# Merged products of the gate and up projections, and tiles moved to multiples of 512 bytes, in a two-layer hybrid decoder trunk

## The chip, the cores and the metric

The kernel runs on one core of one Trainium2 chip. The metric is device time in microseconds, as the median of several runs. The kernel before was measured three times. All matrix work runs on TensorE, called PE in the profile, whose weight loads are listed apart as PEld. VectorE is DVE, ScalarE is ACT, GpSimd is POOL, and SP issues the transfers of the weights.

## What is computed

The reference is a trunk of two layers over 256 tokens of width 1024, in float32. Each layer is a half-weighted SwiGLU, a mixer and another half-weighted SwiGLU, each behind an RMS norm. The four feed-forward parts, each with a hidden width of 2816, are where the change works:

```
def swiglu(h, w_gate, w_up, w_down):
    return (jax.nn.silu(h @ w_gate) * (h @ w_up)) @ w_down

for layer in range(DEPTH):
    x = x + FFN_RES * swiglu(rms_norm(x, pre_norm[layer]), pre_w_gate[layer], ...)
    h = rms_norm(x, mix_norm[layer])
    x = x + (ssd_mla_mixer(h, ...) if layer % 2 == 0 else swa_gla_mixer(h, ...))
    x = x + FFN_RES * swiglu(rms_norm(x, post_norm[layer]), post_w_gate[layer], ...)
```

Mixer 0 joins a state-space scan with latent attention, mixer 1 a sliding-window attention with gated linear attention.

## The kernel before

**Two parts for every operand.** A float32 value is held as two float32r parts, hi (the value rounded by a cast on ACT) and lo (the rest, a subtraction on DVE). A product of an activation h and a weight w is the sum of three matmuls: h-hi by w-hi, h-lo by w-hi and h-hi by w-lo. Each matmul has a weight load of its own on TensorE (the stationary operand, 128 by 128) and then a moving operand whose columns stream through.

**The weights** come in the order of their use through `Stream.load` (line 68). Each slot is a tile of 128 partitions by up to 1024 columns, 512 KB: SP starts its transfer into one of 4 raw buffers, ACT casts it into one of 8 hi buffers (line 78), and DVE subtracts into one of 8 lo buffers (line 80). POOL takes a third of the subtractions where a share is given (line 82), which the loop over column tiles and the down projection of the feed-forward part don't do.

**A feed-forward part** is `ffn` (line 340). The first 512 columns of gate and up are made by tokens (`in_tok`, lines 274 to 276): the stationary operand is a 128-token block of the activations and the moving operand 512 columns of the weight. The other 18 column tiles of 128 columns each go through `in_ch` (lines 284 to 293): the stationary operand is a 128 by 128 block of the weight, the moving operand all 256 tokens. For each of the 8 k tiles, `in_ch` issues hi by xh, hi by xl and lo by xh, into one half of a PSUM bank; gate has one half and up the other, so a column tile fills one of the 4 banks that products with weights take in turn. Then ACT takes the silu of the gate half (line 364), DVE multiplies by the up half (line 365), and `split` makes the two parts of the result on ACT (line 229) and DVE (line 230). The down projection is `proj` (line 295): for each of the 22 k tiles the stationary operand is a block of activations and the moving one 512 columns of the weight, three matmuls (lines 308 to 310) for each of two token tiles and two halves. After the first token tile ends, its norm runs under the second one's products (`norm`, line 243); `split` there works on four k tiles at once, 512 elements to a partition. The turned result is hT, two tiles of hi (four k tiles each) and two of lo.

**Order.** The engines' queues are in order. A scheduler sets the order from the program and a timing model, so a piece that waits holds what stands behind it on its engine.

**Place of the tiles in SBUF.** A pool lays its tiles one after another. Before, the pool "sb" holds everything but the weights, large and small tiles mixed, and the pool of the weights follows it. In the built program every large tile of group "b" (hT, gains, x, half of the lo parts of the hidden activations) and every raw, hi and lo weight buffer begins 128 bytes past a multiple of 512. The large tiles of group "a" (the hi parts of the hidden activations and the others of the lo parts, the outputs of the attention, the turned outputs of the scan) begin 192 bytes past one. A 128 by 128 float32r block is 512 bytes to a partition, and blocks lie at steps of 512 bytes within these tiles, so a stationary block has the start of its tile: 128 past for the weights' blocks and for hT, 192 past for the hidden activations.

Of the kernel before, what the change touches and what calls it, by code (L numbers as in the profile page):

```python
# [6 lines left out]
dt = mybir.dt  # L7
# [21 lines left out]
# log1p(e) / e on [0, 1], least maximum relative error 5e-9  # L29
# [4 lines left out]
# columns of the row of small vectors that is broadcast to all partitions  # L34
# [7 lines left out]
# columns of the square constants  # L42
# [3 lines left out]
def two_pi_parts():  # L46
    """2 pi as 12-bit pieces and the rest"""
    parts, rest = [], TWO_PI
    for _ in range(3):
        m, e = np.frexp(rest)  # L50
        p = float(np.ldexp(np.floor(m * 4096), e - 12))
        parts.append(p)
        rest -= p
    return parts + [rest]


class Stream:
    """The weights in the order of their use. Each slot is [128, w]; a load
    brings one or two slots in one transfer, and each is split exactly into
    two float32r parts."""  # L60
# [7 lines left out]
    def load(self, widths, share=0.0):  # L68
        """share: of the subtractions, the part that Pool takes over from DVE"""
# [18 lines left out]
class Net:  # L88
    def __init__(self, tc, sb, wp, ps, args):
        self.tc, self.nc = tc, tc.nc  # L90
        self.sb, self.ps, self.args = sb, ps, args
        self.st = Stream(self.nc, wp, args["w"], 4, 8)
        self.k = 0

# [5 lines left out]
    def blk(self, shape, name, dtype=F32, grp="b"):  # L100
        """a tile from the common pools; those of a group are given out in the order of the program,
        so that work that may run ahead of other work has a group of its own"""
        size = int(np.prod(shape[1:])) * 4
        tag, bufs = next((t, n) for t, m, n in self.POOLS[grp] if size <= m)
        return self.sb.tile(shape, dtype, tag=tag, name=f"{name}_{self.uid()}", bufs=bufs)
# [4 lines left out]
    def bank(self, shape, name):  # L110
        """for the products with weights"""
# [11 lines left out]
    def order(self, later, earlier):  # L123
        """both on one engine: `later` is issued after `earlier`"""
# [15 lines left out]
    def constants_more(self):  # L140
# [13 lines left out]
        # the silu of the convolution is taken as (tanh(v / 2) + 1) * (v / 2): halves, exactly  # L154
        nc.vector.tensor_scalar(out=self.conv, in0=self.conv, scalar1=0.5, scalar2=None, op0=ALU.mult)
        # gains of the no-position part of q and k, on k alone
# [3 lines left out]
        # masks added to scores in PSUM  # L160
        self.identb = self.small([P, P], "identb", BF16)
# [8 lines left out]
        # distances of the window's positions, with a large number outside of it  # L170
# [61 lines left out]
    def power(self, out, in_):  # L232
        """in_ ** -0.5"""
        self.pow = self.nc.gpsimd.tensor_tensor(out=out, in0=in_, in1=self.mhalf[:, :in_.shape[1]], op=ALU.pow)

    def new_hT(self):
        return [[self.blk([P, 4, S], f"hT{s}{j}", F32R) for j in range(2)] for s in "hl"]

    @staticmethod
    def hk(hT, k):  # L240
        return hT[0][k // 4][:, k % 4, :], hT[1][k // 4][:, k % 4, :]

    def norm(self, x, t, g, hT):
        """token tile t of the RMS norm of x, turned: columns of t in hT"""
# [10 lines left out]
        for h in range(2):  # L255
# [5 lines left out]
            c = (slice(None), slice(None), slice(t * P, (t + 1) * P))  # L261
            self.split(hT[0][h][c], hT[1][h][c], tp)
# [3 lines left out]
    def mm_tok(self, out, at, ks, t, w, first, last):  # L266
        """out[tokens of t, cols] += a^T w over the k tiles ks, w their (hi, lo)"""
# [10 lines left out]
    def in_tok(self, out, hT, t, w, n, per):  # L278
        """out = h w for token tile t; w: slots of `per` k tiles, n columns each"""
# [4 lines left out]
    def in_ch(self, out, hT, w):  # L284
        """out [128 columns of the weight, 256 tokens]"""
# [8 lines left out]

    def proj(self, nk, at, x, scale, after, turn=TURN, lag=LAG, share=0.0):
        """x[t] += scale * (a w), a = at(k, t) (hi, lo) [128, 128]. The first token tile ends `lag`
        k tiles before the second, so that after(t, half) runs under the second's products; what
        TensorE has to do in it is put between these from their half `turn` on."""
# [33 lines left out]
        # at the end of all the second tile ends by halves  # L332
# [7 lines left out]
    def ffn(self, hT, x, after):  # L340
# [17 lines left out]
        for f in range(G0, NF):  # L358
            w = st.load([D, D])
            b = self.bank([P, 2, S], "gu")  # L360
            for j in range(2):
                self.in_ch(b[:, j, :], hT, w[j])
            sg = self.blk([P, n0], "sg")[:, :S]
            nc.scalar.activation(out=sg, in_=b[:, 0, :], func=AF.Silu)
            nc.vector.tensor_tensor(out=sg, in0=sg, in1=b[:, 1, :], op=ALU.mult)  # L365
# [8 lines left out]
    def log1p_exp(self, v, e, name):  # L374
        """e = log1p(exp(-|v|)); returns the tile that holds it"""
# [10 lines left out]
    def attend(self, t, pt, v, den, out):  # L386
        """out: (hi, lo) [128, 4, 128] of the turned outputs of 8 heads;
        pt(block, h) [128 k, 128 q], v(block, h) [128 k, 64]"""
# [14 lines left out]
    def turn_probs(self, p, n, name):  # L403
        """p(h) [128 q, 128 k] for 8 heads -> [128 k, 8, 128 q]"""
# [13 lines left out]
    def conv_silu(self, c, b, out):  # L418
        """causal convolution and silu of channel tile c, b [128, 256] in PSUM"""
# [11 lines left out]
    def apply_rope(self, out, x, t, which, nh):  # L431
        """out, x [128, nh, 2, 16] (out may not be x)"""
# [9 lines left out]
    def mixer0(self, hT, x, after):  # L442
# [3 lines left out]
        # --- dt, q_a, kv_c, k_pe, by tokens  # L446
# [33 lines left out]
        # --- B and C of the state space, [state, token]  # L480
# [9 lines left out]
        # --- q and k of the latent attention  # L490
# [5 lines left out]
        for t in range(2):  # L496
# [15 lines left out]
            # 96^-1/2 / rms = (sum of squares + 96 eps)^-1/2  # L512
# [40 lines left out]
        # --- dt = softplus, a = -dt exp(a_log), its running sum by chunk  # L553
        e = self.small([P, 2, 16], "dte")
        l1 = self.log1p_exp(dtv, e, "dtl")
        dts = self.small([P, 2, 16], "dts")
# [10 lines left out]
        # the same by rows, to come back on all partitions  # L567
# [12 lines left out]
        # --- scores and softmax  # L580
# [33 lines left out]
        # --- decays of a chunk, masked products C B  # L614
        dec = self.small([P, 16], "dec")

        def decays(t):
# [10 lines left out]
            for g in range(4):  # L628
# [3 lines left out]
                if t == g == 0:  # the rows arrive while DVE still has a convolution to do  # L632
# [10 lines left out]
        # --- x of the state space: by tokens, times dt and times D  # L643
# [21 lines left out]
        # --- outputs of the scan onto x D  # L665
# [10 lines left out]
        # --- gate, by halves of the channels  # L676
# [9 lines left out]
        # --- grouped norm  # L686
# [26 lines left out]
        # the state after the first chunk, and what the second takes from it  # L713
# [32 lines left out]
    def mixer1(self, hT, x, after):  # L746
# [5 lines left out]
        # --- k, v, gate rank and q, by tokens  # L752
# [12 lines left out]
        for t in range(2):  # L765
# [26 lines left out]
            # 64^-1/2 / rms = (sum of squares + 64 eps)^-1/2  # L792
# [8 lines left out]
        # --- window attention  # L801
# [6 lines left out]
        def scores(t):  # L808
# [5 lines left out]
            for j in range(8 // n):  # L814
                # the heads of a bank are all even or all odd: their operands lie on the same partitions
# [32 lines left out]
        # --- log gates and their running sums, [channel, token]  # L848
# [8 lines left out]
        # --- keys, queries, values of the linear attention  # L857
# [18 lines left out]
        # --- decays, on keys and queries  # L876
# [39 lines left out]
        # --- states of the linear attention  # L916
# [19 lines left out]
        # --- gate  # L936
# [189 lines left out]
```

## Time and profile before

| | us |
|---|---|
| median of 3 runs | 1070.3 |
| fastest and slowest of them | 1069.41, 1070.86 |
| span of the profiled execution, first to last instruction | 1067.0 |
| PE busy, share of the span | 1039.9, 97% |
| PEld busy | 937.8, 88% |
| DVE busy | 634.1, 59% |
| ACT busy | 517.9, 49% |
| POOL busy | 204.0, 19% |

The runs' times are those of whole executions, and the span lies within one: no own time of the profiled execution is given apart from its span, which is 3.3 us under the median of the runs. The ends of matmuls are modelled, so that each shows longer than its turn in the stream: neighbours overlap. How often PE starts a matmul is read from the start times in the timeline.

### The profile page before, as it was taken

The page shows a single profiled execution, that of the slowest core. Times are in us where ns is not written, and L with a number is a line of the kernel's source. Part 1 is how long each engine was busy: PE and PEld are TensorE (multiplying, and loading weights), DVE is VectorE, ACT ScalarE, POOL GpSimd, SP SyncE. Part 2 cuts the span into 40 slices and gives each one's busy share as a digit, 9 for nine tenths or more (in the row PEclk, how much of TensorE's full clock was granted, in tenths as well). Part 3 has the DMA queues.
Part 4 walks back from the last instruction along what each step waited for, and adds up shares of the span by engine and source line. Part 5 has one row for each costly group of instructions (what it writes and reads, how often), then busy time and mean ns, then how long its engine had stood idle before and what let it go on. Part 6 is the DMA issues. An engine that isn't in the chain of part 4 may idle for free.

```text
span 1067.0 us, 17171 instructions
## 1 busy us (share of the span) xinstructions
PE 1039.9 (97%) x6729; PEld 937.8 (88%) x6729; DVE 634.1 (59%) x890; ACT 517.9 (49%) x836; POOL 204.0 (19%) x215
## 2 busy tenths in 40 slices
PE   5999999998999999999999999999999999999998
PEld 4899988897998789999887999988887778999986
DVE  5855554587887666555435655544588576555441
ACT  6544443377755355444334544443365355444430
POOL 6100000368656340000013000000362240000000
PEclk9999999999999999999999999999999999999999
DMA  8765655454444257555554655554463246665451
GB/s 291 254 203 180 184 172 189 134 197 146 158 140 168 109 178 250 185 178 184 189 182 156 218 185 189 179 181 157 158 197 121 99 141 192 189 190 180 150 186 40
DMA packets 52097, 186.08 MB, mean 174 GB/s; under 512 B 5911, under 2 KB 5928, under 8 KB 52016
## 3 DMA queue, kind: packets, MB, share of 16 engines
q1 hardware_dynamic: 49248, 176.58, 49.7%
q0 software_dynamic: 2048, 6.83, 1.7%
q10 hardware_dynamic: 720, 1.57, 0.4%
q8 instruction: 53, 0.87, 0.3%
q14 instruction: 28, 0.23, 0.1%
HBM read 183.89 MB, written 1.06 MB: 173 GB/s over the span
## 4 chain that ended last, share of the span: by engine, by line
PE 87%; DMA 4%; DVE 4%; issue 2%; POOL 1%; ACT 1%; DVEq 0%; POOLq 0%; ACTq 0%; SPq 0%
PE p_gu L292 13%; PE p_gu L291 13%; PE p_gu L293 13%; PE p_acc L310 9%; PE p_acc L309 9%; PE p_acc L308 9%; DVE wl L80 2%; DMA raw<-in_w 1%; PE p_u L276 1%; PE p_u L275 1%; PE p_u L274 1%; DMA E<-acs_rows 1%; PE p_g L275 1%; PE p_g L276 1%; PE p_g L274 1%
## 5 line engine op out<-in xcount | busy, mean ns | idle before, releaser
L80 DVE TENSOR_TENSOR wl<-raw,wh 128x1024 fp32r<-128x1024 f32 (+4 forms) x341 | 400.9, 1185 | 303.6 <-ACT wh L78 302.3
L78 ACT CAST wh<-raw 128x1024 fp32r<-128x1024 f32 (+3 forms) x341 | 350.6, 1035 | 375.4 <-issue 133.9
L292 PE MATMUL p_gu<-hTl,wh 128*128 128x256 f32 x1152 | 326.6, 283 | 0.0
L293 PE MATMUL p_gu<-hTh,wl 128*128 128x256 f32 x1152 | 326.5, 283 | 0.0
L291 PE MATMUL p_gu<-hTh,wh 128*128 128x256 f32 x1152 | 326.3, 283 | 0.0
L82 POOL TENSOR_TENSOR wl<-raw,wh 128x320 fp32r<-128x320 f32 (+3 forms) x109 | 126.2, 1168 | 568.4 <-ACT wh L78 562.5
L291 PEld LDWEIGHTS p_gu<-hTh,wh 128*128 128x128 f32 x1152 | 221.3, 192 | 0.2
L292 PEld LDWEIGHTS p_gu<-hTl,wh 128*128 128x128 f32 x1152 | 221.2, 192 | 0.2
L293 PEld LDWEIGHTS p_gu<-hTh,wl 128*128 128x128 f32 x1152 | 221.3, 192 | 0.0
L310 PE MATMUL p_acc<-wl,acth 128*128 128x512 f32 x352 | 139.8, 397 | 0.0
L309 PE MATMUL p_acc<-wh,actl 128*128 128x512 f32 x352 | 139.6, 397 | 0.0
L308 PE MATMUL p_acc<-wh,acth 128*128 128x512 f32 x352 | 138.4, 395 | 0.0
L309 PEld LDWEIGHTS p_acc<-wh,actl 128*128 128x128 f32 x352 | 66.3, 188 | 15.9
L308 PEld LDWEIGHTS p_acc<-wh,acth 128*128 128x128 f32 x352 | 66.3, 188 | 15.7
L310 PEld LDWEIGHTS p_acc<-wl,acth 128*128 128x128 f32 x352 | 66.1, 188 | 15.2
L316 DVE SCALAR_TENSOR_TENSOR x<-p_acc,x 128x512 f32<-128x512 f32 x24 | 16.4, 685 | 37.9 <-PE p_acc L310 37.8
L291 PE MATMUL p_xbc<-hTh,wh 128*128 128x256 f32 x128 | 36.8, 288 | 1.2 <-DVE cv L425 1.2
L293 PE MATMUL p_xbc<-hTh,wl 128*128 128x256 f32 x128 | 36.7, 287 | 0.0
L292 PE MATMUL p_xbc<-hTl,wh 128*128 128x256 f32 x128 | 36.5, 285 | 0.0
L229 ACT CAST acth<-sg 128x256 fp32r<-128x256 f32 x72 | 29.0, 402 | 5.4 <-DVE sg L365 5.4
L230 DVE TENSOR_TENSOR actl<-sg,acth 128x256 fp32r<-128x256 f32 x72 | 30.3, 420 | 1.9 <-ACT acth L229 1.9
L249 ACT ACTIVATE junk<-x 128x512 f32<-128x512 f32 x24 | 15.2, 632 | 30.3 <-DVE x L316 26.6
(368 smaller groups left out, 1378.1 us busy)
## 6 DMA issues: line engine op xcount, KB each, us to landing
raw<-in_w SPq DMA_DIRECT2D x326, 512.0 KB, 4.2
gain<-in_gains POOLq DMA_DIRECT2D x5, 512.0 KB, 6.1
E<-acs_rows POOLq DMA_DIRECT2D x4, 512.0 KB, 6.4
raw<-in_w SPq DMA_DIRECT2D x4, 400.0 KB, 2.9
raw<-in_w SPq DMA_DIRECT2D x4, 288.0 KB, 2.8
raw<-in_w SPq DMA_DIRECT2D x3, 384.0 KB, 3.6
raw<-in_w SPq DMA_DIRECT2D x4, 272.0 KB, 2.7
out<-x ACTq DMA_DIRECT2D x4, 256.0 KB, 2.1
```

The costliest lines, as they stand in the source:

```text
L78: nc.scalar.copy(out=hi, in_=raw)
L80: nc.vector.tensor_tensor(out=lo[:, :cut], in0=raw[:, :cut], in1=hi[:, :cut].bitcast(F32), op=ALU.subtract)
L82: nc.gpsimd.tensor_tensor(out=lo[:, cut:], in0=raw[:, cut:], in1=hi[:, cut:].bitcast(F32), op=ALU.subtract)
L229: self.nc.scalar.copy(out=hi, in_=src)
L230: self.nc.vector.tensor_tensor(out=lo, in0=src, in1=hi.bitcast(F32), op=ALU.subtract)
L274: mm(out, ah, wh, start=first and i == 0, stop=False)
L291: mm(out, hi[:, cs], xh, start=k == 0, stop=False)
L292: mm(out, hi[:, cs], xl, start=False, stop=False)
L293: mm(out, lo[:, cs], xh, start=False, stop=k == KT - 1)
L308: first = nc.tensor.matmul(o, ah, w[0][:, s], start=k == 0, stop=False)
L309: nc.tensor.matmul(o, al, w[0][:, s], start=False, stop=False)
L310: nc.tensor.matmul(o, ah, w[1][:, s], start=False, stop=k == nk - 1)
```

## The change

There are three parts. All comments are taken out as well, which leaves the program the same.

1. `in_ch2` takes the place of `in_ch` for the 18 column tiles of each feed-forward part (the mixers keep `in_ch`). For each k tile the weight's hi block is loaded once and hi and lo of the tokens pass it as one moving operand of 512 columns, into a whole bank: the products with xh in the first half, those with xl in the second. The lo block's product with xh, 256 columns, adds to the first half. Gate and up so have a bank each, and a column tile takes two of the four banks. The two halves are added behind it: ACT copies the second half out, DVE adds the first.
2. For that hT becomes four tiles, each of two k tiles with hi and lo side by side. `norm` splits in pieces of two k tiles, 256 elements to a partition.
3. The pools are laid in another order: a small pool "edge" of 384 bytes (two small tiles), then the large tiles ("big"), then the weights, then all other small tiles. In the built program every large tile and every weight buffer then begins at a multiple of 512 bytes, and so does every stationary block cut from one in steps of 512 bytes.

```diff
     def new_hT(self):
-        return [[self.blk([P, 4, S], f"hT{s}{j}", F32R) for j in range(2)] for s in "hl"]
+        return [self.blk([P, 2, 2, S], f"hT{j}", F32R) for j in range(4)]
...
     def hk(hT, k):
-        return hT[0][k // 4][:, k % 4, :], hT[1][k // 4][:, k % 4, :]
+        return hT[k // 2][:, k % 2, 0, :], hT[k // 2][:, k % 2, 1, :]
...
-            c = (slice(None), slice(None), slice(t * P, (t + 1) * P))
-            self.split(hT[0][h][c], hT[1][h][c], tp)
+            c = slice(t * P, (t + 1) * P)
+            for j in range(2):
+                o = hT[2 * h + j]
+                self.split(o[:, :, 0, c], o[:, :, 1, c], tp[:, 2 * j:2 * j + 2, :])
...
+    def in_ch2(self, out, hT, w):
+        mm = self.nc.tensor.matmul
+        hi, lo = w
+        for k in range(KT):
+            cs = slice(k * P, (k + 1) * P)
+            mm(out, hi[:, cs], hT[k // 2][:, k % 2], start=k == 0, stop=k == KT - 1, skip_group_check=True)
+            mm(out[:, 0, :], lo[:, cs], self.hk(hT, k)[0], start=False, stop=k == KT - 1, skip_group_check=True)
...
             w = st.load([D, D])
-            b = self.bank([P, 2, S], "gu")
+            v = self.blk([P, 2, S], "sg")
             for j in range(2):
-                self.in_ch(b[:, j, :], hT, w[j])
-            sg = self.blk([P, n0], "sg")[:, :S]
-            nc.scalar.activation(out=sg, in_=b[:, 0, :], func=AF.Silu)
-            nc.vector.tensor_tensor(out=sg, in0=sg, in1=b[:, 1, :], op=ALU.mult)
+                b = self.bank([P, 2, S], "gu"[j])
+                self.in_ch2(b, hT, w[j])
+                nc.scalar.copy(out=v[:, j, :], in_=b[:, 1, :])
+                nc.vector.tensor_tensor(out=v[:, j, :], in0=v[:, j, :], in1=b[:, 0, :], op=ALU.add)
+            sg = v[:, 0, :]
+            nc.scalar.activation(out=sg, in_=sg, func=AF.Silu)
+            nc.vector.tensor_tensor(out=sg, in0=sg, in1=v[:, 1, :], op=ALU.mult)
             self.split(act[0][f // 4][:, f % 4, :], act[1][f // 4][:, f % 4, :], sg)
...
-    with tc.tile_pool(name="sb", bufs=1) as sb, tc.tile_pool(name="w", bufs=1) as wp, \
+    with tc.tile_pool(name="edge", bufs=1) as edge, tc.tile_pool(name="big", bufs=1) as big, \
+            tc.tile_pool(name="w", bufs=1) as wp, tc.tile_pool(name="sb", bufs=1) as sb, \
             tc.tile_pool(name="ps", bufs=1, space=bass.MemoryType.PSUM) as ps:
```

On PE, where gate ends and up begins in the first column tile (p_gu is its bank; hTh and hTl are the parts of the tokens, wh and wl those of the weight), the order before is:

```order
L291 MATMUL p_gu_410<-hTh_3_70,wh_0_400 128x256
L292 MATMUL p_gu_410<-hTl_5_72,wh_0_400 128x256
L293 MATMUL p_gu_410<-hTh_3_70,wl_0_401 128x256
L291 MATMUL p_gu_410<-hTh_2_69,wh_1_406 128x256
L292 MATMUL p_gu_410<-hTl_4_71,wh_1_406 128x256
L293 MATMUL p_gu_410<-hTh_2_69,wl_1_407 128x256
```

The same place with the change (p_g and p_u are now banks of their own; the turn of an earlier result stands between):

```order
L305 MATMUL p_g_425<-hT_5_78,wh_0_414 128x512
L121 MATMUL m_ffT_345<-sq,sg_342 128x128 x4
L306 MATMUL p_g_425<-hT_5_78,wl_0_415 128x256
L305 MATMUL p_u_444<-hT_2_75,wh_1_420 128x512
L306 MATMUL p_u_444<-hT_2_75,wl_1_421 128x256
```

Three matmuls of 256 columns for a k tile have become one of 512 and one of 256.

On DVE, in the middle of the loop over column tiles (wl is the lo part of a weight still to be used, sg the tile of the result, actl its lo part), a turn of the loop before is:

```order
L230 TENSOR_TENSOR actl_52_219<-sg_987,acth_46_213 128x256
L80 TENSOR_TENSOR wl_1_1265<-raw_1_1262,wh_1_1264 128x1024
L365 TENSOR_TENSOR sg_1053<-sg_1053,p_gu_1004 128x256
L80 TENSOR_TENSOR wl_0_1325<-raw_0_1322,wh_0_1324 128x1024
L230 TENSOR_TENSOR actl_52_219<-sg_1053,acth_46_213 128x256
```

With the change:

```order
L378 TENSOR_TENSOR sg_974<-sg_974,p_g_975 128x256
L230 TENSOR_TENSOR actl_51_233<-sg_919,acth_45_227 128x256
L80 TENSOR_TENSOR wl_1_1191<-raw_1_1188,wh_1_1190 128x1024
L378 TENSOR_TENSOR sg_974<-sg_974,p_u_994 128x256
L381 TENSOR_TENSOR sg_974<-sg_974 128x256
L80 TENSOR_TENSOR wl_0_1240<-raw_0_1237,wh_0_1239 128x1024
```

A turn has two additions (L378) more; the result of a column tile is split one slot later than before.

On DVE, where the norm after a feed-forward part runs (p_acc are the banks of the down projection, x the running sum, m_nrm the turned norm), the order before is:

```order
L80 TENSOR_TENSOR wl_0_2073<-raw_0_2070,wh_0_2072 128x384
L80 TENSOR_TENSOR wl_1_2080<-raw_1_2077,wh_1_2079 128x384
L230 TENSOR_TENSOR hTl_41_208<-m_nrm_1962,hTh_39_206 128x4x128
L316 SCALAR_TENSOR_TENSOR x_65<-p_acc_1590,x_65 128x512
L230 TENSOR_TENSOR hTl_42_209<-m_nrm_1970,hTh_40_207 128x4x128
```

With the change:

```order
L230 TENSOR_TENSOR hT_38_220<-m_nrm_1778,hT_38_220 128x2x128
L329 SCALAR_TENSOR_TENSOR x_71<-p_acc_1406,x_71 128x512
L230 TENSOR_TENSOR hT_39_221<-m_nrm_1778,hT_39_221 128x2x128
L230 TENSOR_TENSOR hT_40_222<-m_nrm_1788,hT_40_222 128x2x128
L329 SCALAR_TENSOR_TENSOR x_71<-p_acc_1407,x_71 128x512
L80 TENSOR_TENSOR wl_0_1911<-raw_0_1908,wh_0_1910 128x384
L230 TENSOR_TENSOR hT_41_223<-m_nrm_1788,hT_41_223 128x2x128
```

Each subtraction of four k tiles has become two of two.

## Rows read from the trace of the kernel before

**Rows 1.** The page: span, busy time, granted clock, and the chain by engine.

```profile
span 1067.0 us, 17171 instructions
PE 1039.9 (97%) x6729; PEld 937.8 (88%) x6729; DVE 634.1 (59%) x890; ACT 517.9 (49%) x836; POOL 204.0 (19%) x215
...
PEclk9999999999999999999999999999999999999999
...
PE 87%; DMA 4%; DVE 4%; issue 2%; POOL 1%; ACT 1%; DVEq 0%; POOLq 0%; ACTq 0%; SPq 0%
```

**Rows 2.** Windows by stage: us; PE, PEld, DVE, ACT, POOL busy; clock; DMA share, GB/s.

```profile
0.00:30.00 30.00, 17.62 (x72) 13.12 (x73) 18.38 (x32) 17.52 (x27) 18.59 (x30) 1.00 0.83 294
...
48.00:149.00 101.00, 101.00 (x823) 100.00 (x822) 55.82 (x73) 47.38 (x71) 0.00 (x0) 1.00 0.63 196
149.00:206.00 57.00, 57.00 (x251) 46.03 (x250) 26.36 (x27) 21.81 (x26) 6.60 (x7) 1.00 0.46 142
206.00:376.00 170.00, 162.05 (x1073) 147.87 (x1072) 133.22 (x234) 104.75 (x219) 100.09 (x106) 1.00 0.45 157
...
765.00:868.00 103.00, 102.19 (x604) 83.69 (x603) 70.64 (x124) 54.61 (x125) 39.82 (x35) 1.00 0.43 140
```

**Rows 3.** Timeline of PE, column tiles: start us, us, engine line op names shapes.

```profile
99.82 0.28 PE L291 MATMUL p_gu<-hTh,wh 128*128 128x256 f32 x1
99.94 0.28 PE L292 MATMUL p_gu<-hTl,wh 128*128 128x256 f32 x1
...
102.94 0.28 PE L293 MATMUL p_gu<-hTh,wl 128*128 128x256 f32 x1
```

**Rows 4.** Timeline of PE, first column block of the first feed-forward part.

```profile
33.56 0.39 PE L275 MATMUL p_u<-wh,hTl 128*128 128x512 f32 x1
...
35.83 0.39 PE L276 MATMUL p_u<-wl,hTh 128*128 128x512 f32 x1
```

**Rows 5.** Timeline of PE, down projection.

```profile
160.08 0.39 PE L309 MATMUL p_acc<-wh,actl 128*128 128x512 f32 x1
...
163.81 0.39 PE L310 MATMUL p_acc<-wl,acth 128*128 128x512 f32 x1
```

**Rows 6.** Timeline of PE, four turns of a 128 by 128 block in mixer 0.

```profile
288.50 0.60 PE L121 MATMUL m_pT<-sq,p 128*128 128x128 f32 x4
```

**Rows 7.** Groups of PE by form: names, shapes, count | busy us, mean ns | idle before.

```profile
L291 PE MATMUL p_gu<-hTh,wh 128*128 128x256 f32 x1152 | 326.3, 283 | 0.0
L310 PE MATMUL p_acc<-wl,acth 128*128 128x512 f32 x352 | 139.8, 397 | 0.0
...
L275 PE MATMUL p_g<-wh,hTl 128*128 128x512 f32 x64 | 25.9, 404 | 3.9 <-DVE hTl L230 3.9
...
L121 PE MATMUL m_pT<-sq,p 128*128 128x128 f32 x48 | 7.2, 273 | 0.0
```

**Rows 8.** Groups of DVE, whole span: lo parts of the tokens in the norms.

```profile
L230 DVE TENSOR_TENSOR hTl<-m_nrm,hTh 128x512 fp32r<-128x512 f32 x24 | 16.0, 681 | 11.1 <-ACT hTh L229 11.1
```

**Rows 9.** Groups of DVE between 60 and 140 us, 14 column tiles.

```profile
L80 DVE TENSOR_TENSOR wl<-raw,wh 128x1024 fp32r<-128x1024 f32 x28 | 34.3, 1226 | 37.0 <-ACT wh L78 37.0
L230 DVE TENSOR_TENSOR actl<-sg,acth 128x256 fp32r<-128x256 f32 x14 | 5.9, 419 | 0.0
L365 DVE TENSOR_TENSOR sg<-sg,p_gu 128x256 f32<-128x256 f32 x14 | 5.8, 415 | 0.0
```

**Rows 10.** Groups of ACT in the same stretch.

```profile
L78 ACT CAST wh<-raw 128x1024 fp32r<-128x1024 f32 x28 | 29.3, 1047 | 43.1 <-issue 25.0 <-PE p_gu L292 18.1
L229 ACT CAST acth<-sg 128x256 fp32r<-128x256 f32 x14 | 5.6, 402 | 0.0
L364 ACT ACTIVATE sg<-p_gu 128x256 f32<-128x256 f32 x14 | 5.3, 378 | 0.0
```

**Rows 11.** Waits of PE: line, who was waited for, us in total, times, longest.

```profile
PE p_g L275 <- DVE hTl L230: 3.9, 5, 1.6
```

**Rows 12.** DMA issues: line, queue, count, KB each, median us to landing.

```profile
raw<-in_w SPq DMA_DIRECT2D x326, 512.0 KB, 4.2
```

More of the change, by code (lines that the diff above doesn't have):

```diff
@@ L88, with __init__ @@
 class Net:
-    def __init__(self, tc, sb, wp, ps, args):
+    def __init__(self, tc, edge, big, sb, wp, ps, args):
         self.tc, self.nc = tc, tc.nc
-        self.sb, self.ps, self.args = sb, ps, args
+        self.edge, self.big, self.sb, self.ps, self.args = edge, big, sb, ps, args
         self.st = Stream(self.nc, wp, args["w"], 4, 8)
@@ L104, in blk @@
         tag, bufs = next((t, n) for t, m, n in self.POOLS[grp] if size <= m)
-        return self.sb.tile(shape, dtype, tag=tag, name=f"{name}_{self.uid()}", bufs=bufs)
+        return self.big.tile(shape, dtype, tag=tag, name=f"{name}_{self.uid()}", bufs=bufs)
     def small(self, shape, name, dtype=F32, bufs=1):
@@ L159, in constants_more @@
         nc.vector.tensor_tensor(out=self.kgain[:64], in0=kq[:64, 0:1], in1=kq[:64, 1:2], op=ALU.mult)
-        self.identb = self.small([P, P], "identb", BF16)
+        self.identb = self.edge.tile([P, P], BF16, tag="identb", name="identb", bufs=1)
         nc.scalar.copy(out=self.identb, in_=self.ident)
@@ L555, in mixer0 @@
         l1 = self.log1p_exp(dtv, e, "dtl")
-        dts = self.small([P, 2, 16], "dts")
+        dts = self.edge.tile([P, 2, 16], F32, tag="dts", name="dts", bufs=1)
         nc.vector.scalar_tensor_tensor(out=dts, in0=dtv, scalar=0.0, in1=l1, op0=ALU.max, op1=ALU.add)
@@ L983, in run @@
         nc = self.nc
-        x = [self.sb.tile([P, D], F32, tag=f"x{t}", name=f"x{t}", bufs=1) for t in range(2)]
+        x = [self.big.tile([P, D], F32, tag=f"x{t}", name=f"x{t}", bufs=1) for t in range(2)]
         nc.sync.dma_start(out=x[0], in_=self.args["x"][:P, :])
@@ L1020, in program @@
 def program(tc, args, out, steps=STEPS):
-    with tc.tile_pool(name="sb", bufs=1) as sb, tc.tile_pool(name="w", bufs=1) as wp, \
+    with tc.tile_pool(name="edge", bufs=1) as edge, tc.tile_pool(name="big", bufs=1) as big, \
+            tc.tile_pool(name="w", bufs=1) as wp, tc.tile_pool(name="sb", bufs=1) as sb, \
             tc.tile_pool(name="ps", bufs=1, space=bass.MemoryType.PSUM) as ps:
-        Net(tc, sb, wp, ps, args).run(out, steps)
+        Net(tc, edge, big, sb, wp, ps, args).run(out, steps)
 def by_k(w):
```

## The prediction

> **What bounds the kernel now.** I read the page first: the span is 1067.0 us, PE is busy for 97% of it at a granted clock of 1.000 throughout, and the chain that ended last runs over PE for 87% [rows 1]. The windows by stage say where that holds: in the column tiles (48 to 149 us) and the down projection (149 to 206) PE has no idle time at all, while DVE and ACT are idle for nearly half or more; in mixer 0 (206 to 376) DVE, ACT and POOL carry 133, 105 and 100 of 170 us, so several engines take turns there; the first 30 us are a stretch of transfers, at 294 GB/s [rows 2]. So in the feed-forward parts what counts is how often PE starts a matmul, and "busy" doesn't tell that, since the shown durations overlap. Start times do.
>
> In the column tiles 26 turns pass from 99.82 to 102.94 us: **120.0 ns** for 256 columns [rows 3]. At the granted 2.4 GHz, 256 columns are 106.7 ns, so a turn has 13.3 ns over. In the first column block 10 turns pass from 33.56 to 35.83 us: 227.0 ns for 512 columns, which are 213.3 ns, so 13.7 over [rows 4]. In the down projection 16 turns pass from 160.08 to 163.81 us: 233.1 ns, 19.8 over [rows 5]. The surplus doesn't grow with the columns. It goes with the start of the stationary block: 128 bytes past a multiple of 512 in the first two cases, 192 past in the third. That is 0.104, 0.107 and 0.103 ns for each byte: proportional, and a line through them comes to nought at 0. The moving operand starts 128 past in all three, so by these rows it explains no difference.
>
> A second floor is seen where the moving operand is short. Four turns of 128 columns take 0.60 us [rows 6], of which the last's own 273 ns [rows 7] is drain: (600 - 273) / 3 = **109 ns** each, twice what 128 columns take at 2.4 GHz. I read it as the time of a weight load, which a matmul can't undercut. A load lies beside every matmul (823 and 822 in the second window [rows 2]).
>
> **The change part by part.**
>
> *Column tiles.* 1152 k steps [rows 7] of three matmuls take 3 x 120.0 = 360 ns. After: one of 512 columns and one of 256, both from aligned blocks. With the surplus gone the first takes 213.3, and the second 109, by the floor of the load that runs beside it: 322.3 ns. 1152 x 37.7 = **43.4 us**. Bounds: if the surplus stays at 13.3, 226.6 + 120 = 346.6, 15.4 us; if the load is no floor, 320, 46.1 us.
>
> *Down projections.* 3 x 352 matmuls [rows 7] lose 19.8 ns each: **20.9 us**; between 0 (nothing goes) and that.
>
> *First column blocks.* 64 for each of six kinds of matmul [rows 7], 384 in all, lose 13.3 ns: 5.1 us. A quarter lies in the first 30 us, which transfers set [rows 2]: **3.8 us**; between 0 and 5.1.
>
> *Mixers.* 1073 + 604 matmuls in the two windows [rows 2]. All of them at 13.3 ns would be 22 us; below it is 0, since a shorter matmul may only wait longer for DVE or POOL. Many are short and at the 109 ns floor already. I take **8 us**, about a third.
>
> *New work behind a column tile.* Two copies on ACT (like the silu that reads the same bank, 378 ns) and two additions on DVE (like the product there, 415 ns) [rows 9, 10]. DVE has per tile 2 x 1.226 + 0.415 + 0.419 = 3.29 us, after the change 4.12; ACT has 2 x 1.047 + 0.402 + 0.378 = 2.87, then 3.63 [rows 9, 10]. A turn of the loop is 16 x 322.3 = 5.16 us. Both fit. DVE's 37.0 us of idle time there is a wait for ACT's cast [rows 9], and that waits in part for PE to let go of a hi buffer [rows 10]: they refill buffers used up to four tiles later. I cost it at nothing. What hides it is the 1.0 us per tile left on DVE and the banks: gate's bank comes round after three more half tiles, 7.7 us, while the cast, a subtraction, the copy and the addition in front of its release sum to 3.1 us. Without that cover each tile would pay the 0.79 us of a copy and an addition, 57 us over 72 tiles.
>
> *Norms.* A lo part of four k tiles takes 681 ns [rows 8], and the two pieces that replace it 2 x 419 [rows 9]: 0.16 us more, and about as much on ACT. PE waited for such parts five times, 3.9 us in all [rows 11]. Five times 0.3 us: **1.5 us** lost; between 3 and, since the first piece is ready earlier, a gain of 1. POOL and SP get nothing new. SP's transfers will start sooner: 1 MB per 5.16 us is 203 GB/s against 196 in the second window, with 294 seen in the first 30 us [rows 2], and 4 raw buffers cover 4 x 2.58 = 10.3 us against 4.2 us to landing [rows 12].
>
> *Sum.* 43.4 + 20.9 + 3.8 + 8 - 1.5 = 74.6 us. The durations are of an execution whose span is 1067.0 us, so 992.4 by its span; with the 3.3 us between that span and the median of 1070.3, **995.7**. I say 996.
>
> By the Trainium skill, page "TensorE: Matmul & The Clock Gate", section "Back-to-back issue gap", a warm matmul starts every N / 2.4 + 2.5 ns: 109.2 for 256 columns and 215.8 for 512, and no address enters. The trace shows 10.8 ns more than that in rows 3. If 2.5 ns is what remains after the change, the sum would be 325.0 ns a k step and some 6 us less gain, 1002 us, my estimate from that page.
>
> **The rivals.**
>
> *The surplus is a cost of each matmul and its load, whatever the address.* For it: 13.3 and 13.7 ns for 256 and 512 columns alike. Against it: 19.8 in the down projection, with the same columns as the 13.7. Then the count alone gains: 1152 matmuls fewer, 13.3 ns each, 15.4 us: **1055 us**. The Trainium skill, page "SBUF — State Buffer", section "Operand start alignment", asks of a start only that it is a multiple of the element size, and says that this is about legality and not speed; a reader who took that for all there is would stand with this rival.
>
> *Half of it.* The surplus depends on the place of the moving operand in the memory as well, or two blocks that both start at 0 meet in another way: the rows hold only two starts, so a line through them is no proof of the third. Half the gain of the aligned parts (20.9 + 3.8 + 8 + 28) / 2 beside the 15.4: 45 us, **1025 us**.
>
> *DVE becomes the bound, and the kernel slower.* Place: the loop over column tiles, on DVE's queue. Each addition stands behind a copy on ACT, and that copy behind a cast there; if DVE stands still for both, twice per tile, it needs 4.12 + 2 x (1.047 + 0.378) = 6.97 us per tile, against 5.76 now. 72 tiles: 87 us lost in place of 43.4 gained, so 1070 + 87 - 31 = **1126 us**. It decides from 5.16 + 74.6 / 72 = 6.20 us per tile, that is where DVE's new waiting passes 2.1 us per tile. For it: DVE already waits 37.0 us for casts in 14 tiles [rows 9]. Against it: that wait is for buffers which PE holds, four tiles ahead, and shrinks when DVE has more to do.
>
> **How the numbers follow.** The forecast has 0.80, the fixed cost 0.08, half of it 0.07, DVE's bound 0.05. The forecast's own range: all upper bounds (46.1 + 20.9 + 5.1 + 22 + 1) give 975, but that needs every mixer matmul to gain, so I take 11 there: 985. The low ends (a remaining 2.5 ns, nothing from the mixers, 3 us in the norms) give 1070 - 40 - 18 - 3 + 3 = 1012. Between 980 and 1012 lie most of the 0.80; taking in the half case, up to 1030, leaves out the fixed cost, DVE's bound and some tails, about 0.18. What a measurement of this kernel can tell from no change is about 0.2%, 2 us. Faster by more than that: the first three cases, 0.95, less 0.02 for a mixture with DVE's waits that comes out even: 0.93. Within 0.2%: 0.02. Slower: 0.05.
>
> **What would show it.** In the column tiles of the new profile, starts alternate 213 and 109 ns apart, a tile takes 5.16 us, and PE has no idle time there; turns in the down projection are 213 to 216 ns; mixer 0 shrinks by 5 us or so. If the turns are 227 and 120, the start of a block isn't what costs. If they are right but gaps of PE end with a wait for DVE's wl or a bank, the new work is not hidden. If PE's turns in the down projection stay at 233 while the column tiles gain, the layout of group "a" isn't what I take it for. A time above 1030 or under 980 makes the prediction wrong, and so does a right time with other turns.

## The result and the profile after

The changed kernel takes **1050.79 us** (median, 1049.95 to 1052.69), the kernel before 1070.58 in the same runs: 0.9816 of it, 95% interval 0.9801 to 0.983. That is 19.8 us faster, where 74.6 were forecast. The time lies above the range, and it is the rival "a cost of each matmul, whatever the address" (1055) that came nearest.

The page of the kernel after, the lines of [rows 1]:

```profile
span 1049.2 us, 15263 instructions
...
PE 1026.1 (98%) x5577; PEld 878.5 (84%) x5577; DVE 692.5 (66%) x1058; ACT 561.3 (53%) x1004; POOL 205.0 (20%) x215
...
PE 91%; DVE 5%; issue 1%; POOL 1%; DMA 1%; ACT 1%; POOLq 0%; DVEq 0%; ACTq 0%
```

1152 matmuls are gone (6729 to 5577), and yet PE is busy for a larger share of the span than before, 98% for 97%. The windows by stage, columns as in [rows 2]:

```profile
0.00:30.00 30.00, 20.51 (x81) 15.93 (x82) 19.22 (x38) 18.41 (x32) 18.67 (x30) 1.00 0.85 295
48.00:143.00 95.00, 95.00 (x543) 83.48 (x542) 68.28 (x107) 57.05 (x104) 0.00 (x0) 1.00 0.66 206
143.00:199.00 56.00, 56.00 (x253) 46.43 (x252) 26.65 (x29) 22.03 (x28) 6.33 (x7) 1.00 0.47 147
199.00:369.00 170.00, 163.10 (x1065) 148.25 (x1064) 134.20 (x234) 103.23 (x221) 101.34 (x105) 0.98 0.47 156
```

In the column tiles PE still has no idle time (95.00 of 95.00), with DVE up from 55% to 72%: the new copies and additions cost nothing, as forecast. So the missing gain is inside PE's own stream. The timeline of PE there, first feed-forward part (start us, us, engine, line, operation, names):

```profile
99.76 0.39 PE L305 MATMUL p_g<-hT,wh 128*128 128x512 f32 x1
99.99 0.28 PE L306 MATMUL p_g<-hT,wl 128*128 128x256 f32 x1
100.11 0.39 PE L305 MATMUL p_g<-hT,wh 128*128 128x512 f32 x1
...
102.88 0.39 PE L305 MATMUL p_u<-hT,wh 128*128 128x512 f32 x1
```

Nine k steps from 99.76 to 102.88: 346.7 ns each, 230 and 117, where 213.3 and 109 were forecast and 360 stood before [rows 3]. That is one surplus less, not three. And in the second part:

```profile
440.57 0.40 PE L305 MATMUL p_u<-hT,wh 128*128 128x512 f32 x1
...
440.92 0.40 PE L305 MATMUL p_u<-hT,wh 128*128 128x512 f32 x1
...
441.28 0.40 PE L305 MATMUL p_u<-hT,wh 128*128 128x512 f32 x1
...
443.40 0.40 PE L305 MATMUL p_g<-hT,wh 128*128 128x512 f32 x1
```

Eight k steps take 2.83 us: 353.8 ns each. Parts 1 and 3 run at 347, parts 2 and 4 at about 354, from the second column tile to the last. The first column block (nine turns) and the down projection (13 turns):

```profile
33.03 0.39 PE L278 MATMUL p_u<-wh,hT 128*128 128x512 f32 x1
...
35.07 0.39 PE L277 MATMUL p_u<-wh,hT 128*128 128x512 f32 x1
```

```profile
154.71 0.39 PE L323 MATMUL p_acc<-wl,acth 128*128 128x512 f32 x1
...
157.66 0.39 PE L321 MATMUL p_acc<-wh,acth 128*128 128x512 f32 x1
```

226.7 ns for the first, as in [rows 4]: moving its stationary block to a multiple of 512 changed nothing. 226.9 for the second, which was 233.1 [rows 5]: a gain of 6.2, not 19.8, down to the value that the first column block always had.

Where the 17.8 us between the two spans lie, as the time from PE's first start in a stage to its last, in the two profiled executions (for a mixer, from the last start of the down projection before it to the first of the column block behind it; the forecast's -1.5 for the norms has no row of its own):

| us | before | after | forecast gain | gain |
|---|---|---|---|---|
| from PE's first start to the first column tile | 30.0 | 27.8 | | 2.2 |
| column tiles, four parts | 416.3 | 405.0 | 43.4 | 11.3 |
| down projections, four | 248.1 | 241.4 | 20.9 | 6.7 |
| first column blocks of parts 2 to 4 | 70.9 | 69.7 | 3.8 (all four) | 1.1 |
| mixers with their norms | 286.8 | 290.2 | 8 | -3.4 |

### The profile page after: what moved, and what is told of

It is laid out like the page before. It is cut to its first block, busy times and chain, and to the rows that moved or that the text cites. A ratio compares the mean times of both kernels' runs of the same rounds, so it can differ in the third digit from the quotient of the medians.

```text
span 1049.2 us, 15263 instructions
## 1 busy us (share of the span) xinstructions
PE 1026.1 (98%) x5577; PEld 878.5 (84%) x5577; DVE 692.5 (66%) x1058; ACT 561.3 (53%) x1004; POOL 205.0 (20%) x215
## 4 chain that ended last, share of the span: by engine, by line
PE 91%; DVE 5%; issue 1%; POOL 1%; DMA 1%; ACT 1%; POOLq 0%; DVEq 0%; ACTq 0%
PE p_g L305 13%; PE p_u L305 13%; PE p_acc L322 9%; PE p_acc L323 9%; PE p_acc L321 9%; PE p_u L306 7%; PE p_g L306 7%; DVE wl L80 2%; PE p_g L278 2%; PE p_g L279 1%; PE p_u L279 1%; PE p_u L278 1%; PE p_g L277 1%; PE p_u L277 1%; PE m_att_o L409 1%
## 5 line engine op out<-in xcount | busy, mean ns | idle before, releaser
L305 PE MATMUL p_u<-hT,wh 128*128 128x512 f32 x576 | 205.1, 395 | 0.0
L305 PE MATMUL p_g<-hT,wh 128*128 128x512 f32 x576 | 204.9, 395 | 0.0
L306 PE MATMUL p_u<-hT,wl 128*128 128x256 f32 x576 | 161.9, 281 | 0.0
L306 PE MATMUL p_g<-hT,wl 128*128 128x256 f32 x576 | 161.6, 281 | 0.0
L305 PEld LDWEIGHTS p_g<-hT,wh 128*128 128x128 f32 x576 | 108.0, 187 | 25.4
L305 PEld LDWEIGHTS p_u<-hT,wh 128*128 128x128 f32 x576 | 108.0, 188 | 25.2
L306 PEld LDWEIGHTS p_g<-hT,wl 128*128 128x128 f32 x576 | 108.8, 189 | 0.2
L306 PEld LDWEIGHTS p_u<-hT,wl 128*128 128x128 f32 x576 | 108.8, 189 | 0.0
L294 PE MATMUL p_xbc<-hT,wh 128*128 128x256 f32 x128 | 36.8, 287 | 0.1
L295 PE MATMUL p_xbc<-hT,wh 128*128 128x256 f32 x128 | 36.5, 285 | 0.0
L296 PE MATMUL p_xbc<-hT,wl 128*128 128x256 f32 x128 | 36.3, 283 | 0.0
```

The source lines that it names most:

```text
L294: mm(out, hi[:, cs], xh, start=k == 0, stop=False)
L295: mm(out, hi[:, cs], xl, start=False, stop=False)
L296: mm(out, lo[:, cs], xh, start=False, stop=k == KT - 1)
L305: mm(out, hi[:, cs], hT[k // 2][:, k % 2], start=k == 0, stop=k == KT - 1, skip_group_check=True)
L306: mm(out[:, 0, :], lo[:, cs], self.hk(hT, k)[0], start=False, stop=k == KT - 1, skip_group_check=True)
```

## The experiments

**The places alone.** The kernel before with the new pools, and its old products and hT:

```
...
-    with tc.tile_pool(name="sb", bufs=1) as sb, tc.tile_pool(name="w", bufs=1) as wp, \
+    with tc.tile_pool(name="edge", bufs=1) as edge, tc.tile_pool(name="big", bufs=1) as big, \
+            tc.tile_pool(name="w", bufs=1) as wp, tc.tile_pool(name="sb", bufs=1) as sb, \
...
```

> The kernel before with the new places of the tiles alone (every large tile and weight buffer at a multiple of 512 bytes), products and hT as before. Theory F (a matmul with its weight load costs about 13 ns over its columns at a start of 0 as well as 128, and some 6 ns more at 192): the column tiles keep 120 ns a turn, the first blocks 227, the down projections fall from 233 to 227, four times 1.6 us; with a little in the mixers 1063 us. Theory R (the layout did nothing, the down projection of the changed kernel gained by its new hT or order): 233 stays, 1070 us. Theory P, of the prediction (surplus proportional to the start): 107 to 109 and 213, which the changed kernel has already spoken against: 1015 us.

1063.31 us, 0.9941 of the kernel before (0.9919 to 0.9964). Its timeline of PE in the column tiles (ten turns) and the down projection (16 turns):

```profile
99.75 0.28 PE L293 MATMUL p_gu<-hTh,wl 128*128 128x256 f32 x1
...
100.95 0.28 PE L291 MATMUL p_gu<-hTh,wh 128*128 128x256 f32 x1
```

```profile
159.67 0.39 PE L310 MATMUL p_acc<-wl,acth 128*128 128x512 f32 x1
...
163.30 0.39 PE L308 MATMUL p_acc<-wh,acth 128*128 128x512 f32 x1
```

120.0 ns and 226.9. The column tiles gain nothing from blocks at multiples of 512; the down projections gain all that they gain in the change.

**The products alone.** The change with the pools of before (weights and hT 128 past, group "a" 192 past):

```
-    with tc.tile_pool(name="edge", bufs=1) as edge, tc.tile_pool(name="big", bufs=1) as big, \
-            tc.tile_pool(name="w", bufs=1) as wp, tc.tile_pool(name="sb", bufs=1) as sb, \
+    with tc.tile_pool(name="sb", bufs=1) as sb, tc.tile_pool(name="w", bufs=1) as wp, \
...
-        Net(tc, edge, big, sb, wp, ps, args).run(out, steps)
...
+        Net(tc, sb, sb, sb, wp, ps, args).run(out, steps)
```

> The changed kernel with the tiles at their old places (weights and hT 128 past a multiple of 512, group a 192 past). F: a k step of the column tiles takes 347 ns, as with aligned tiles, or 353 in the two parts where the changed kernel showed that; the down projection stays at 233; 11 to 15 us faster than before, 1055 to 1059 us. R: the down projection falls to 227 here, 1051 us. If the merging pays only with aligned blocks: 360 a k step, 1070 us.

1061.13 us, 0.9909 (0.9888 to 0.9931). The down projections stay as they were. In the column tiles seven k steps take 2.47 us, 353 ns each, and here all four parts do:

```profile
99.92 0.40 PE L305 MATMUL p_g<-hT,wh 128*128 128x512 f32 x1
...
102.39 0.40 PE L305 MATMUL p_g<-hT,wh 128*128 128x512 f32 x1
```

Places and products together take 1.84% off and singly 0.59% and 0.91%. The remaining 0.34%, some 3.6 us, is not far above the intervals of these ratios, but the starts show it directly: the four parts' column tiles sum to 408.7 us here and to 405.0 in the change, where parts 1 and 3 run at 347 ns a step.

**All large tiles 192 past.** The change with 192 bytes in front of everything, so that stationary blocks and moving operands move together:

```
+        pad = edge.tile([P, 48], F32, tag="pad", name="pad", bufs=1)
+        self.nc.gpsimd.memset(pad, 0.0)
```

> The changed kernel with 192 bytes put in front, so that every large tile and weight buffer begins 192 past a multiple of 512. F: each matmul costs about 6 ns more than in the changed kernel: a k step 360 ns, the down projection 233, the first blocks 233; 15 + 7 + 3 us, 1074 to 1077 us. R: no change against the changed kernel, 1051 us. If only the weight blocks or only the hidden activations mind the start, one of the two parts.

1050.49 us, one run. Nine k steps of the column tiles in the first part, and 14 turns of the down projection:

```profile
99.32 0.39 PE L307 MATMUL p_g<-hT,wh 128*128 128x512 f32 x1
...
102.44 0.39 PE L307 MATMUL p_u<-hT,wh 128*128 128x512 f32 x1
```

```profile
159.80 0.39 PE L324 MATMUL p_acc<-wh,actl 128*128 128x512 f32 x1
...
162.97 0.39 PE L323 MATMUL p_acc<-wh,acth 128*128 128x512 f32 x1
```

That is 230 and 117 ns in the column tiles of parts 1 and 3, and 226 to 227 in the down projections. No spacing changed. By the forecast's proportion every matmul would have paid 19.8 ns over its columns here, 233 and 126 ns. That reading falls: where a block starts does not by itself set the surplus.

**Isolated products.** Streams of 24 equal products, with the starts of the stationary and of the moving operand set one by one.

```
+            for i in range(turns):
...
+                so = (s + 512 * (i % 4)) // es
+                mo = (4096 if es == 2 else 8192) // es + (m + 2048 * (i % 2) * es // 4) // es
+                nc.tensor.matmul(b[:sc, :c], w[:rows, so:so + sc], w[:rows, mo:mo + c], start=i == 0, stop=i == turns - 1,
...
```

> Only products of fixed blocks, one kind after another, and none of the trunk's work: 24 turns of each kind back to back, read as the spacing of starts. F: 512 columns of float32r take 227 ns at every start of the stationary block that is a multiple of 128 bytes (0, 128, 256, 384) and 233 at 64, 192, 320, 448; the moving operand's start changes nothing; 256 columns 120 and 384 columns 173; a bfloat16 block 220. P: 213 at 0, rising by 0.104 ns a byte. Rival M (the moving operand's start counts as well): the turns differ between its starts. Rival W (the surplus is the time of the block's last part to be loaded): 64 or 32 stationary columns have less than 13 ns over.

Four of the streams in the timeline of PE; the stationary block and the moving operand begin, past a multiple of 512: at 192 and 128; at 128 and 128; at 192 and 0; and at 0 and 0 in bfloat16:

```profile
134.94 5.30 PE L111 MATMUL c<-wr 128*128 128x512 f32 x22
140.53 5.17 PE L111 MATMUL c<-wr 128*128 128x512 f32 x22
57.30 5.20 PE L111 MATMUL c<-wr 128*128 128x512 f32 x22
209.69 5.35 PE L111 MATMUL c<-wb 128*128 128x512 bf16 x24
```

Less the last one's own 0.39 us and divided by 21 (23): 234, 228, 229 and 216 ns. By the start times of the later 20 of each stream, the means are 233.3, 227.3, 228.9 and 215.8. The streams of one width from 256 to 512 columns with a whole 128 by 128 block, all but the first of the run (which begins with turns of 427 ns), as surplus over columns / 2.4:

| stationary minus moving start, modulo 256 | float32r surplus, ns |
|---|---|
| 0 (both starts 0, 64, 128 or 192, or 256 apart; 256, 384 or 512 columns) | 13.1 to 14.6 |
| 16, 32, 64 or 96 | 19.9 to 20.6 |
| 128 | 18.6 to 19.4 |
| 192 | 15.4 to 15.7 |
| 224, 240 | 20.0, 18.0 |
| bfloat16, stationary starts 0, 32, 64 and 128, moving start 0, 256 or 512 columns | 2.5 |

So the surplus has two parts. **13.3 ns belong to each float32r matmul** of 256 to 512 columns with a load beside it, wherever in these streams its block starts. Up to seven more go with the **difference** between the two operands' starts. A stream of 128 columns turns every 111.7 ns, close to the 109 of [rows 6]. A stationary block of 64 or 32 columns had no smaller surplus (16.5, 18.4).

The kernel before had a difference of 0 in its column tiles (128 and 128) and of 64 in most of its down projections (192 and 128): 13.3 and 20.0, within 0.2 ns the two values that the forecast read as a proportion. There is one exception. Of the six lo tiles of the hidden activations four, not half, lie in group "b": the lo products of k tiles 8 to 21 in a down projection have their stationary block at 128 and the weight at 128. The timeline of PE there, 15 turns:

```profile
185.27 0.40 PE L309 MATMUL p_acc<-wh,actl 128*128 128x512 f32 x1
...
188.77 0.40 PE L309 MATMUL p_acc<-wh,actl 128*128 128x512 f32 x1
```

The mean is still 233.3 ns, though every third product has a difference of 0; product by product the rule would give 231.1. So it holds for streams of one difference, and where differences are mixed it doesn't add up by the product. Why is open.

Why float32r pays is not shown either; windows of 4.2 us in two streams with both operands at equal starts, float32r and bfloat16, show only that the records of its loads are longer:

```profile
141.00:145.20 4.20, 4.20 (x20) 3.48 (x19) 0.00 (x0) 0.00 (x0) 0.00 (x0) 1.00 0.00 0
210.50:214.70 4.20, 4.20 (x22) 1.89 (x20) 0.00 (x0) 0.00 (x0) 0.00 (x0) 1.00 0.02 4
```

3.48 us for 19 loads, 183 ns each, against 94 in bfloat16. Such a record is not the time that the next load must wait: in the column tiles of the kernel before, loads of 192 ns stand 120 ns apart.

**The difference, in the kernel.** 64 bytes between the large tiles and the weights of the change:

```
+            tc.tile_pool(name="gap", bufs=1) as gap, tc.tile_pool(name="w", bufs=1) as wp, tc.tile_pool(name="sb", bufs=1) as sb, \
...
+        tc.nc.gpsimd.memset(gap.tile([P, 16], F32, tag="gap", name="gap", bufs=1), 0.0)
```

> 64 bytes are left free between the large tiles and the weights, so that the weights start 64 past a multiple of 512 and the large tiles at one. Theory D (the surplus goes with the difference between the start of the stationary block and that of the moving operand, modulo 256: 13.3 ns at 0, about 20 at 64, 15.5 at 192, by the isolated products): the column tiles, with a difference of 64, take 233.3 + 126.7 = 360 ns a k step, 13.3 more than 347, some 13 us in all (1152 x 13.3, less what the slow cycle took already); the down projections and the first column blocks, with 192, take 228.8 in place of 227.0, 1440 x 1.8 = 2.6 us. Some 1066 us, 0.996 of the kernel before: nearly the whole gain is gone. Rival S (the start of the stationary block alone, proportional, over a fixed 13.3 ns): the column tiles +6.7 a matmul as well, but the down projections, whose stationary block still starts at a multiple of 512, stay at 227.0: 1064 us. Rival N (no start matters to 13.3 ns and it is the place in the memory that gained): 1050.8 us, 347 and 227.0.

1057.58 us, 0.9898 (0.9877 to 0.9918): 6.8 us of the gain lost to 64 bytes by the two medians, some 9 by the two ratios (the kernel before took 1069.14 us beside this run, 1070.58 beside the change). Four k steps of the column tiles, and 18 turns of the down projection:

```profile
99.87 0.40 PE L305 MATMUL p_u<-hT,wh 128*128 128x512 f32 x1
...
101.28 0.40 PE L305 MATMUL p_g<-hT,wh 128*128 128x512 f32 x1
```

```profile
159.71 0.39 PE L321 MATMUL p_acc<-wh,acth 128*128 128x512 f32 x1
...
163.83 0.39 PE L321 MATMUL p_acc<-wh,acth 128*128 128x512 f32 x1
```

228.9 ns in the down projections, whose stationary blocks still start at multiples of 512: 228.8 was Theory D's number, and 227.0 that of Rival S, which falls. In the column tiles a step is 353 ns in all four parts, not 360. That it is not just the slow step of parts 2 and 4 is seen in single starts: here every step is 235 and 118 ns, there three steps take turns (232 and 118, 240 and 120, 236 and 114). So a start that differs costs there too, but in the alternation of two widths its price is 6 ns a step and not twice 6.7, and against the slow step nothing. That size was missed: 1066 us were forecast.

**What makes 347 or 354.** In five column tiles of each part some of the gate's products change places:

```
+    def swapped(*ks):
...
+            res += [(c, k) for c in ("lH" if k in ks else "Hl")]
...
+    return {0: plain, 7: swapped(4), 10: swapped(3, 5), 13: swapped(2, 3, 4), 16: swapped(2, 4, 6),
+            19: [("H", k) for k in range(KT)] + [("l", k) for k in range(KT)]}
```

> In column tiles 7, 10, 13, 16 and 19 of each part the gate's products change places in one to all of the k steps (no work is added); the others are as in the change. Theory K (which of the two steps runs is set by how the alternation was entered, and stays until something disturbs it): the k steps between two swaps are all 347 ns or all about 353.7, and at least one swap makes a slow part fast or a fast one slow. Rival M (it belongs to the part): first and third part 347, second and fourth 353.7 throughout, whatever the swaps. The time is within 4 us of 1050.8 by either.

1053.76 us, one run. The timeline of PE around the first swap, in column tile 7 of the first part:

```profile
53.14 0.39 PE L321 MATMUL p_u<-hT,wh 128*128 128x512 f32 x1
...
55.57 0.39 PE L321 MATMUL p_g<-hT,wh 128*128 128x512 f32 x1
55.80 0.40 PE L323 MATMUL p_g<-hT,wl 128*128 128x256 f32 x2
56.03 0.63 PE L321 MATMUL p_g<-hT,wh 128*128 128x512 f32 x2
...
57.32 0.40 PE L321 MATMUL p_u<-hT,wh 128*128 128x512 f32 x1
...
60.14 0.40 PE L321 MATMUL p_g<-hT,wh 128*128 128x512 f32 x1
```

Seven k steps before it take 2.43 us, 347 ns each; eight behind it 2.82, 353. Parts 1, 2 and 3 were at 347 up to the swap and near 353 from it to the end, across four more swaps; part 4 was slow throughout. Part 2, slow in the change, began fast here, with the same instructions in front. So it is not the part, its tiles or its banks: an alternation of two widths falls into one of two rhythms when it is entered or disturbed, and keeps it. Rival M falls. Nor is it the place of the tiles: the products alone, at 128 and 128, ran slow in all four parts, while four isolated alternations of 512 and 256 columns, with both operands at 0, 64, 128 or 192, all ran at 347 ns a pair. What in PE holds the rhythm, and why a part enters one or the other, was not found.

**Widths in groups.** Eight products of 512 columns, then eight of 256:

```
             mm(out, hi[:, cs], hT[k // 2][:, k % 2], start=k == 0, stop=k == KT - 1, skip_group_check=True)
+        for k in range(KT):
+            cs = slice(k * P, (k + 1) * P)
             mm(out[:, 0, :], lo[:, cs], self.hk(hT, k)[0], start=False, stop=k == KT - 1, skip_group_check=True)
```

> In a column tile the eight products of 512 columns come first, then the eight of 256; nothing else is changed. Theory K (the 353.7 ns of a k step in the second and fourth feed-forward part come from the alternation of two widths, which can fall into a cycle of three k steps): runs of one width have no such cycle, 227 and 120 ns throughout, 347 ns a k step in all four parts; the second and fourth part are 288 x 6.7 = 1.9 us shorter each, 3.9 us in all, 1047 us, 0.978 of the kernel before. Rival M (the slower step belongs to these parts: their tiles, banks or transfers): still about 353.7 there, 1050.8 us.

1049.63 us, 0.9827 (0.9805 to 0.9849): not told apart from the change. Two starts of such a tile half in the first part, and two in the second:

```profile
102.10 2.00 PE L305 MATMUL p_u<-hT,wh 128*128 128x512 f32 x8
...
104.90 2.00 PE L305 MATMUL p_g<-hT,wh 128*128 128x512 f32 x8
```

```profile
440.48 2.00 PE L305 MATMUL p_g<-hT,wh 128*128 128x512 f32 x8
...
443.27 2.00 PE L305 MATMUL p_u<-hT,wh 128*128 128x512 f32 x8
```

2.80 and 2.79 us for eight k steps, 349 to 350 ns in all four parts: no slow rhythm, as Theory K has it, but two to three ns a step go at the changes of width, so that the four stages sum to 403.8 us against 405.0. The expected 3.9 us were 1.2, and those are below what this comparison can tell.

## Why the prediction was wrong

**The step that failed** is the reading of the surplus: "It goes with the start of the stationary block", "proportional, and a line through them comes to nought at 0". All four gains of the sum used it. It rested on two starts, 128 and 192, that in those rows came with two differences, 0 and 64. The isolated products and the change shifted by 192 separate start and difference: at equal starts the surplus is 13.3 ns wherever the block lies, and no layout tried takes that away. The rows held the counter-argument in plain sight, as the rival "half of it" said: two points, and a moving operand that started 128 past in all of them, so that it could not be told whether its place matters. Equally, column tiles and first column blocks of [rows 3, 4] showed 13.3 to 13.7 for twice the columns, the mark of a cost per matmul. And the trace held a row in which only the stationary start moved: the lo products of k tiles 8 to 21, at 128, which by the proportion should have turned in 227 ns, run among the others at a mean of 233.3. The chance of 0.08 for the rival of a cost per matmul was far too small.

*Column tiles, 43.4 us forecast.* Merging takes away one matmul's 13.3 ns per k step, not three: 1152 x 13.3 = 15.4 us, the lower bound given there. 11.3 came, since parts 2 and 4 run at 354 ns: 2 x 288 x 7 ns = 4.0 us given back. The 109 ns put in for the second matmul, as a floor by the load, did not bind: it took 117, above that.

*Down projections, 20.9.* The sign came right by luck: moving every tile to one start also took away the difference, which the forecast did not know of. 1056 x 6.2 = 6.5 us went with the difference of 64 in most of their products, which became 0; 6.7 were measured.

*First column blocks, 3.8.* 227 ns before and after, difference 0 both times: nothing. The 1.1 us there and the 2.2 us ahead of the first column tile have no matmul that turns faster; the places alone had no gain ahead of the first column tile (31.4 us), the products alone had it (27.4).

*Norms, -1.5.* The sign was wrong: the first smaller piece is ready earlier, which stood as the bound on the other side, a gain of 1, and more came. PE's waits for such pieces were 3.9 us [rows 11], 2.3 of them ahead of the first column tile, 0.7 in the third part and 0.9 in the fourth. After:

```profile
PE p_g L278 <- DVE hT L230: 0.6, 1, 0.6
```

Those 3.3 us less are as much as the 1.1 and the 2.2 us above, which by that belong to the norms. The stretch ahead of the first column tile varies by a us or so between runs with the new hT (26.3 us in the change shifted by 192), so the split is not exact.

*New work, 0.* Right: with it DVE waits less for the cast, 19.6 us in 14 tiles for 37.0 [rows 9], between 60 and 135 us:

```profile
L80 DVE TENSOR_TENSOR wl<-raw,wh 128x1024 fp32r<-128x1024 f32 x28 | 34.3, 1225 | 19.6 <-ACT wh L78 19.6
```

The rival in which DVE binds had no part.

*Mixers, +8 forecast, -3.4 measured.* Their products had a difference of 0 already in the stages fed by hT. Mixer 0 went from 178.2 to 180.0 us, mixer 1 from 108.5 to 110.2. In mixer 0 the clock fell twice, to the lower level, 1.2 GHz, behind waits of PE. The windows of the kernel after:

```profile
232.00:244.00 12.00, 9.40 (x54) 8.10 (x52) 11.15 (x24) 8.72 (x19) 10.04 (x11) 0.86 0.44 133
241.00:242.00 1.00, 1.00 (x6) 0.93 (x6) 1.00 (x4) 0.10 (x1) 1.00 (x2) 0.50 1.01 401
352.00:364.00 12.00, 11.38 (x46) 8.67 (x45) 4.58 (x9) 1.17 (x2) 1.20 (x1) 0.86 0.31 114
```

In the profile before, the clock was 1.00 in all of mixer 0 [rows 2]. A mean of 0.86 over 12 us is 3.4 us at half speed, so at most about 1.7 us lost, twice. The wait ahead of the first fall, in the timeline of PE, after and then before:

```profile
240.78 1.94 PE L121 MATMUL m_qT<-sq,qnat 128*96 128x128 f32 x8 [2.34 <-POOL qnat L456]
```

```profile
249.12 0.32 PE L121 MATMUL m_qT<-sq,qnat 128*96 128x128 f32 x1 [1.76 <-POOL qnat L440]
```

The order of events suggests that the longer wait lowers the clock and that this costs mixer 0 its time. Neither is shown, and the other runs speak against both. The products alone had the same wait, 2.34 us, with no fall behind it:

```profile
244.45 0.64 PE L121 MATMUL m_qT<-sq,qnat 128*96 128x128 f32 x4 [2.34 <-POOL qnat L456]
```

```profile
244.00:250.00 6.00, 4.88 (x34) 4.37 (x35) 5.46 (x17) 2.64 (x8) 6.00 (x9) 1.00 0.76 269
```

The places alone took 179.7 us in mixer 0 with no fall in it, the products alone 180.0 with one, the change 180.0 with two. And the fall does not come with the change: of 20 later executions of the kernel before, 17 had a mean clock below 1.000 (0.994 to 0.999), as the four of the change had (0.995 to 0.998). The profiled one before was among the few at 1.000, which may be part of why the spans differ by 17.8 us and the medians by 19.8. What lengthens mixer 0 stays open.

Mixer 1 went to 110.2 us at a granted clock of 1.00; it did so in the run with the products alone (110.4) and not with the places alone (108.0), so it comes with the new products or hT, in an order of the mixers that the scheduler made anew. Which instruction pays was not followed further.

The formula of the Trainium skill, page "TensorE: Matmul & The Clock Gate", section "Back-to-back issue gap", N / 2.4 + 2.5 ns, is given there for an isolated matmul at the higher clock. It is what the bfloat16 streams, with a load beside each matmul, show to the tenth: 215.8 and 109.2. For float32r these runs show N / 2.4 + 13.3, so the measurement decides here and the page's 2.5 does not carry over. The Trainium skill's page "SBUF — State Buffer", section "Operand start alignment", gives its rule for a start as one of legality and not of speed, and says that its runs timed nothing, so it makes no forecast of either result here: a start alone cost nothing (1050.49 us with everything shifted by 192), two starts that differ did (64 bytes, 6.8 us).

## What to carry to other kernels

In float32r, count matmuls: each of 256 to 512 columns carried some 13 ns over its columns here, so a wider moving operand under one load gains that much per matmul saved, and no more. Give the stationary and the moving operand of a product the same start modulo 256 bytes; which start did not matter among those tried. Two operands that vary together in the rows at hand cannot be told apart by a line through two points: before a forecast rests on such a line, look for a row in which only one of them moves, and give the other reading its full chance.

## What was not expected of the hardware

In streams of one kind the float32r surplus follows the difference of two operands' starts modulo 256 bytes (13.3 ns at 0, 20.0 at 64, 19.1 at 128, 15.5 at 192), and bfloat16 has none of it (2.5 at the four stationary starts tried). A stream that alternates 512 and 256 columns can run at 347 or at about 353 ns a pair with the same instructions and the same clock, chosen at its entry or at a disturbance and kept for up to a hundred us; one swap of two products changed it in three parts of four.
